# GpSimd's transfers framed as one packet per DMA engine in a short-sequence attention kernel

## The chip, the cores and the metric

The kernel runs on one core of a Trainium2 chip. The metric is the device time of one execution in microseconds (us). A core has five engines with a queue of instructions each: TensorE (PE) for matmuls, VectorE (DVE), ScalarE (ACT), GpSimd (POOL) and SyncE (SP). Data is moved between HBM and the core's memory (SBUF) by 16 DMA engines. A transfer is asked for by an instruction in the queue of GpSimd or of SyncE. It is then cut into packets on the 16 DMA engines, and a semaphore is raised when each of them is done.

## The reference

There are 32 x 12 = 384 heads of attention with a sequence of 128 and a head dimension of 64, in float32:

```python
scores = scale * np.matmul(q, k.transpose(0, 1, 3, 2))
scores_max = np.max(scores, axis=-1, keepdims=True)
attn = np.exp(scores - scores_max)
attn = attn / (np.sum(attn, axis=-1, keepdims=True) + 1e-8)
return np.matmul(attn, v).astype(np.float32)
```

The kernel reads 37.75 MB (q, k, v in float32), writes 12.58 MB, and converts q, k and v to bfloat16 in the transfer itself. It takes the exponential without subtracting the maximum, and divides at the end.

## The kernel before, in words

**Units.** Eight heads are a unit; there are 48 units. Four units are a super-unit, of which there are 12 (`supers`). Each super-unit has one load of q, one of k, and one of v (a group of v, `vgroups`), each of 1 MB in HBM and 0.5 MB in SBUF.

**Loads.** [...] A row of q or k that goes to one partition is 4096 bytes in HBM and 2048 in SBUF, 256 such rows a load. A row of v is 2048 bytes in HBM and 1024 in SBUF, 512 of them a load. q and k have four buffers each (`NQ`), v has two (`NVB`). So the load of a group of v waits until PE has read the group two before it (L396), and a load of q or k waits until DVE has copied out the one four before it (L406).

**Compute.** For each super-unit DVE pairs rows of q or k (`pair_up`, L250), PE transposes them (L177), and DVE copies the result out of PSUM (L259). PE puts v in the order of its heads (`order_v`, L191), and ACT copies it (`keep_v`, L236). For each unit PE computes the scores (L217), ACT takes the exponential (L241), PE multiplies by v with a column of ones beside it (L228), and DVE takes the reciprocal of the sums (L269) and multiplies (L272). The wait for a load of v sits on ACT, in the copy before the group's first (`v_landing`, L317 and L327).

**Stores.** Outputs are gathered one or two units at a time; a store instruction moves 256 KB. The first 34 units' stores (`own`, L365) are issued by GpSimd (34 transfers), the rest by SyncE (14 transfers), at L384 and L387. A store of two units has two pieces.

**Order.** GpSimd's queue is written out by hand (L446 to L461): loads are sorted by the step that needs them, and after each load of k some stores follow. In a settled round it holds a load of v, one of k, two to four store transfers and a load of q. All of GpSimd's transfers go through one DMA queue. SyncE's stores go through another, on the same 16 DMA engines; they are held back until unit 40 is done (`HELD`).

Of the kernel before, what the change touches and what calls it, by code (L numbers as in the profile page):

```python
# [10 lines left out]
def kernel(  # L11
# [29 lines left out]
    def slabs(t, r):  # L41
        x = t.rearrange("b h s d -> (b h s) d")
        return x.rearrange("(n p r) d -> p n (r d)", p=128, r=r)
# [3 lines left out]
    v_rows, o_rows = slabs(v, RV), slabs(out, RO)  # L47
# [34 lines left out]
    NQ, NVB, NVE, NP, NT, NA = 4, 2, 8, 4, 2, 4  # L82
# [7 lines left out]
    def sb(name, shape, dtype):  # L90
        return ctx.enter_context(nc.sbuf_tensor(name, shape, dtype))
# [9 lines left out]
    v_b = [sb(f"v_b{i}", [128, 4, RV * D], bf16) for i in range(NVB)]  # L101
# [27 lines left out]
    def op(engine, key, emit, deps=(), marks=(), dma=()):  # L129
        o = Op()  # L130
        o.key, o.emit, o.deps, o.marks, o.dma = key, emit, deps, marks, dma
        assert key not in position, key
        position[key], engine_of[key] = len(program[engine]), engine
        program[engine].append(o)

    def counts():
        c = {}
        for name, e in MARKS.items():
            n, at = 0, []
            for o in program[e]:  # L140
                n += name in o.marks
                at.append(n)
            c[name] = at
        return c
# [140 lines left out]
    s_o = [tc.alloc_semaphore(f"s_o{i}") for i in range(8)]  # L285
# [74 lines left out]
    def pieces(c):  # L360

        first = sum(stores[:c])
        return 2 if 1 < stores[c] < supers[of_unit[first]][0] // 4 else 1

    own = [c for c in range(len(stores)) if sum(stores[:c + 1]) <= OWN]  # L365

    def lane(c):

        return c % 4 + (4 if c in own else 0)

    def store(c):
        name = "POOL" if c in own else "SP"
        e = ENGINE[name]
        n = stores[c]
        first = sum(stores[:c])
        R, f = supers[of_unit[first]]
        J = R // 4

        def emit():
            dst = o_rows[:, 2 * f:2 * f + 2 * J, :].rearrange("p (a w) e -> p a w e", a=2)[  # L380
                :, :, first - f:first - f + n, :]
            src = o_sb[c][:].rearrange("p (a w e) -> p a w e", a=2, w=n)
            if pieces(c) == 1:
                e.dma_start(out=dst, in_=src).then_inc(s_o[lane(c)], 16)  # L384
            else:
                for a in range(2):
                    e.dma_start(out=dst[:, a], in_=src[:, a]).then_inc(s_o[lane(c)], 16)  # L387

        last = first + n - 1
        op(name, ("store", c), emit, [("N", last if c in own else max(last, HELD))])  # L390

    def pool_load(kind, x):
        deps = []
        if kind == "v":
            if x >= NVB:
                deps = [("V", sum(vgroups[:x - NVB + 1]) - 1)]  # L396
            n, first = vgroups[x], sum(vgroups[:x])
            op("POOL", ("load", kind, x), lambda: nc.gpsimd.dma_start(  # L398
                out=v_b[x % NVB][:, :n, :], in_=v_rows[:, first:first + n, :],
            ).then_inc(s_v[x % NVB], 16), deps)  # L400
            return
        R, f = supers[x]
        j = "qk".index(kind)
        rows, bufs, sm = ((q_rows, q_b, s_q), (k_rows, k_b, s_k))[j]
        if x >= NQ:
            deps = [("P", t) for t in t_order if t[0] == x - NQ and t[1] == j]  # L406
        n = f * 8 // R

        def emit():
            nc.gpsimd.dma_start(  # L410
                out=bufs[x % NQ][:], in_=rows[R][:, n:n + 2, :]).then_inc(sm[x % NQ], 16)

        op("POOL", ("load", kind, x), emit, deps)

# [41 lines left out]
    for _, kind, x in loads:  # L456
        pool_load(kind, x)
        while kind == "k" and sum(stores[:todo[0] + 1]) <= MIXED * (x - 4) / (len(supers) - 5):
            store(todo.pop(0))
    for c in todo:  # L460
        store(c)  # L461

    c = counts()
# [143 lines left out]
```

## Time and profile before

| | |
|---|---|
| median of 4 executions | 132.86 us (132.22 to 134.71) |
| the profiled execution | 135.14 us, of which the span of its instructions is 133.4 us |
| busy PE, DVE, ACT, POOL | 96.4, 90.9, 73.8, 51.2 us |
| GpSimd's DMA queue | 15584 packets, 27.79 MB written |
| SyncE's DMA queue | 3808 packets, 3.67 MB written |
| HBM | 37.75 MB read, 12.58 MB written |

The profile counts a transfer's bytes where they are written. A load that converts reads twice as many bytes from HBM as it writes to SBUF, so 210 GB/s in a stretch of loads is 420 GB/s at the source. A store reads and writes the same number. "DMA share" is the mean share of time in which packets of the 16 engines were open. Packets on one engine overlap, so it can go over 1.

### The profile page before, as it was taken

Reading aid. Unit: us, or ns where it says so; the run is one execution under the profiler, and the core shown is the slowest. Engines: PE = TensorE matmul, PEld = TensorE weight load, DVE = VectorE, ACT = ScalarE, POOL = GpSimd, SP = SyncE. Lnnn points to the kernel's source line nnn. Section 1 sums busy time; section 2 is a strip of 40 time slices with the busy share of each in tenths; the row PEclk is TensorE's granted clock in tenths of the full one; section 3 lists DMA queues with packets and bytes.
Section 4 is the critical chain, followed back from the end, with each engine's and each line's share of the span. In section 5 each row is a group of like instructions: output and inputs, shape, how many; then the busy total and the mean of one; then the engine's idle time right before and its main releaser. Section 6 shows DMA issues by size and latency. Waiting matters only on the chain. (4 is left out here: it accounts for less than half of the span.)

```text
span 133.4 us, 7089 instructions
## 1 busy us (share of the span) xinstructions
PE 96.4 (72%) x3072; PEld 68.5 (51%) x3072; DVE 90.9 (68%) x214; ACT 73.8 (55%) x97; POOL 51.2 (38%) x75
## 2 busy tenths in 40 slices
PE   0045779885989999769668769698499698887500
PEld 0034457564667776556446546476367466655300
DVE  1154447994698999849929839969656868876810
ACT  0001548538567877287187187486267387778500
POOL 5950006042009077491640590690930697000000
PEclk9999999999599999999999999999968999999975
DMA  2999999999999999999999999999999999999960
GB/s 17 170 198 208 210 211 210 209 211 209 207 213 170 159 269 211 210 358 215 213 355 217 212 286 209 257 317 209 252 323 208 246 321 337 403 338 337 325 227 10
DMA packets 19400, 31.56 MB, mean 237 GB/s; under 512 B 1344, under 2 KB 11072, under 8 KB 19392
## 3 DMA queue, kind: packets, MB, share of 16 engines
q0 software_dynamic: 15584, 27.79, 96.9%
q1 hardware_dynamic: 3808, 3.67, 8.1%
q8 instruction: 4, 0.07, 0.2%
q14 instruction: 4, 0.03, 0.1%
HBM read 37.75 MB, written 12.58 MB: 377 GB/s over the span
## 5 line engine op out<-in xcount | busy, mean ns | idle before, releaser
L241 ACT ACTIVATE attnT<-s_ps 128x1024 bf16<-128x1024 f32 x48 | 49.4, 1030 | 0.4 <-PE s_ps L217 0.3
L236 ACT CAST v_e<-v_ps 128x512 bf16<-128x512 f32 x48 | 28.2, 588 | 38.4 <-DMA v_b<-in_v_dram 19.6
L177 PE MATMUL qk_ps<-ident,pair 128*128 128x128 bf16 x384 | 31.9, 231 | 14.6 <-PEq L478 14.4
L191 PE MATMUL v_ps<-v_b,sel 128*32 128x256 bf16 x768 | 31.4, 286 | 13.1 <-PEq L478 13.1
L272 DVE TENSOR_TENSOR o_sb<-o_ps,recip 128x512 f32<-128x512 f32 (+1 forms) x53 | 34.0, 642 | 4.8
L259 DVE COPY qkT<-qk_ps 128x1024 bf16<-128x1024 bf16 x48 | 32.8, 684 | 5.6 <-PE qk_ps L177 4.6
L177 PEld LDWEIGHTS qk_ps<-ident,pair 128*128 128x128 bf16 x384 | 24.1, 103 | 19.8 <-issue 17.4
L398 POOL DMA_DIRECT2D v_b<-in_v_dram x12 | 9.5, 794 | 59.8 <-PE v_ps L191 59.8
L191 PEld LDWEIGHTS v_ps<-v_b,sel 128*32 128x32 bf16 x768 | 16.8, 98 | 19.5 <-issue 15.2
L228 PE MATMUL o_ps<-v_e,attnT 128*32 128x65 bf16 x1536 | 22.5, 199 | 1.7 <-PEq L478 1.1
L387 POOL DMA_DIRECT2D out_dram<-o_sb x32 | 22.9, 728 | 0.0
L269 DVE RECIPROCAL recip<-o_ps 128x8 f32<-128x8 f32 (+1 forms) x53 | 10.5, 199 | 17.6 <-PE o_ps L228 16.9
L228 PEld LDWEIGHTS o_ps<-v_e,attnT 128*32 128x32 bf16 x1536 | 16.5, 97 | 7.6 <-issue 3.4
L217 PE MATMUL s_ps<-qkT 64*128 64x128 bf16 x384 | 19.5, 222 | 0.8 <-PEq L478 0.6
L217 PEld LDWEIGHTS s_ps<-qkT 64*128 64x128 bf16 x384 | 11.1, 95 | 11.1 <-issue 11.1
L250 DVE COPY pair<-q_b 128x1024 bf16<-128x1024 bf16 x24 | 11.0, 458 | 5.5 <-DMA q_b<-in_q_dram 5.4
L250 DVE COPY pair<-k_b 128x1024 bf16<-128x1024 bf16 x24 | 10.2, 427 | 0.0
L410 POOL DMA_DIRECT2D q_b<-in_q_dram x12 | 9.0, 747 | 1.0 <-SPq L96 1.0
L410 POOL DMA_DIRECT2D k_b<-in_k_dram x12 | 8.6, 720 | 0.0
L236 ACT ACT_TABLE_LOAD x1 | 1.3, 1283 | 12.8 <-DMA v_b<-in_v_dram 12.8
L564 DVE COPY sel<-ident 128x128 bf16<-128x128 bf16 x2 | 0.4, 223 | 1.8 <-POOL ident L539 1.8
L384 POOL DMA_DIRECT2D out_dram<-o_sb x2 | 1.5, 744 | 0.0
(8 smaller groups left out, 1.4 us busy)
## 6 DMA issues: line engine op xcount, KB each, us to landing
out_dram<-o_sb POOLq DMA_DIRECT2D x34, 256.0 KB, 11.1
q_b<-in_q_dram POOLq DMA_DIRECT2D x12, 512.0 KB, 13.9
k_b<-in_k_dram POOLq DMA_DIRECT2D x12, 512.0 KB, 12.8
v_b<-in_v_dram POOLq DMA_DIRECT2D x12, 512.0 KB, 10.5
out_dram<-o_sb SPq DMA_DIRECT2D x14, 256.0 KB, 4.6
```

What stands on the lines that cost most here:

```text
L177: i = nc.tensor.transpose(p[:, :, r4, jj, :], x[:, r].rearrange("p a d -> p (a d)"), ident[:])
L191: x = nc.tensor.matmul(t[r4 * 32:(r4 + 1) * 32, i, :, :], lhsT=pick[:, w * nh + i, jv, :], rhs=v_b[g % NVB][:, :n, (4 * jv + r4) * D:(4 * ...
L217: i = nc.tensor.matmul(t[:, a, h, :], lhsT=x[p, 1, 4 * w + h, :], rhs=x[p, 0, 4 * w + h, :], start=True, stop=True)
L228: y = nc.tensor.matmul(t[h * SO:(h + 1) * SO, a, r * (D + 1):(r + 1) * (D + 1)], lhsT=x[:, a, h, r * SO:(r + 1) * SO], rhs=v_e[m % NVE][:, ...
L236: return nc.scalar.copy(v_e[m % NVE][:, :, :D], v_ps[:].rearrange("p (n e) -> p n e", e=D))
L241: return nc.scalar.activation(out=attnT[u % NA][:].rearrange("p a h (r s j) -> p (a h r) s j", r=4, j=J), in_=s_ps[u % 2][:].rearrange("p ...
L250: return nc.vector.tensor_copy(pair[t_index[t] % NP][:], src[:, 8 * b:8 * b + 8])
L259: return nc.vector.tensor_copy(x.rearrange("p h (r j s) -> p (h r) j s", r=4, j=J)[:, :, 2 * b:2 * b + 2, :].rearrange("p x j s -> p x (j ...
L269: nc.vector.reciprocal(r, o4[:, :, :, D]).then_inc(s_r, 1)
L272: return nc.vector.tensor_mul(o[:, :, w, :].rearrange("p a (r d) -> p a r d", d=D), o4[:, :, :, :D], r.unsqueeze(3).to_broadcast([128, o4. ...
L387: e.dma_start(out=dst[:, a], in_=src[:, a]).then_inc(s_o[lane(c)], 16)
L410: nc.gpsimd.dma_start(out=bufs[x % NQ][:], in_=rows[R][:, n:n + 2, :]).then_inc(sm[x % NQ], 16)
```

## The change

`dma_start` takes an argument, `single_packet`: all that one transfer has on a DMA engine is framed as one packet. It is set for GpSimd's stores (all 34), for the loads of q and k from the fifth super-unit on (16 of 24), and for the groups of v from the fourth on (9 of 12). The first four super-units of q and k and the first three groups of v keep the framing that they have. SyncE's 14 stores keep it too. No instruction, wait, buffer or order changes.

```diff
     def store(c):
         name = "POOL" if c in own else "SP"
         e = ENGINE[name]
+        how = {"single_packet": True} if c in own else {}
...
             if pieces(c) == 1:
-                e.dma_start(out=dst, in_=src).then_inc(s_o[lane(c)], 16)
+                e.dma_start(out=dst, in_=src, **how).then_inc(s_o[lane(c)], 16)
             else:
                 for a in range(2):
-                    e.dma_start(out=dst[:, a], in_=src[:, a]).then_inc(s_o[lane(c)], 16)
+                    e.dma_start(out=dst[:, a], in_=src[:, a], **how).then_inc(s_o[lane(c)], 16)
...
             op("POOL", ("load", kind, x), lambda: nc.gpsimd.dma_start(
-                out=v_b[x % NVB][:, :n, :], in_=v_rows[:, first:first + n, :],
+                out=v_b[x % NVB][:, :n, :], in_=v_rows[:, first:first + n, :], single_packet=x >= 3,
             ).then_inc(s_v[x % NVB], 16), deps)
...
             nc.gpsimd.dma_start(
-                out=bufs[x % NQ][:], in_=rows[R][:, n:n + 2, :]).then_inc(sm[x % NQ], 16)
+                out=bufs[x % NQ][:], in_=rows[R][:, n:n + 2, :], single_packet=x >= 4).then_inc(sm[x % NQ], 16)
```

## The prediction

> **What bounds the kernel now.** I read the page's rows by slice first.
>
> ```profile
> DMA  2999999999999999999999999999999999999960
> GB/s 17 170 198 208 210 211 210 209 211 209 207 213 170 159 269 211 210 358 215 213 355 217 212 286 209 257 317 209 252 323 208 246 321 337 403 338 337 325 227 10
> q0 software_dynamic: 15584, 27.79, 96.9%
> q1 hardware_dynamic: 3808, 3.67, 8.1%
> ```
>
> The DMA engines are full from 3 us to about 128 us, nearly all of it with GpSimd's queue. No compute engine is above 72%. In pure loads the rate is 208 to 213 GB/s written, so 416 to 426 GB/s read, and slices with more stores show more only because a store's bytes count once. The chain of waits reaches back only to 124 us, so I took the list of waits next.
>
> ```profile
> POOL v_b L398 <- PE v_ps L191: 59.8, 10, 12.0
> ACT v_e L236 <- DMA v_b<-in_v_dram: 19.6, 9, 3.2
> DVE pair L250 <- DMA q_b<-in_q_dram: 5.4, 3, 3.1
> ```
>
> ACT waits for a group of v nine times, at most 3.2 us: about once a round. GpSimd's 59.8 us of idle time is the buffer wait that spaces the rounds; its last six v loads start at 47.35, 55.35, 64.57, 74.80, 84.60, 93.58 and 104.52 us, a round of 57.17 / 6 = 9.53 us. Then I asked ACT's timeline where the waiting for loads ends.
>
> ```profile
> 106.06 0.59 ACT L236 CAST v_e<-v_ps 128x512 bf16<-128x512 f32 x1 [2.14 <-DMA v_b<-in_v_dram]
> ...
> 121.35 0.59 ACT L236 CAST v_e<-v_ps 128x512 bf16<-128x512 f32 x1
> ```
>
> At 106.06 us ACT takes up the copy that waited for group 10 of v (the eleventh, landed at 105.70). From there no engine waits for a load. Eight more copies come in 15.29 us, 1.91 us a unit, 7.6 us a super-unit: compute is 1.9 us a round faster than the 9.53 us of DMA. So the time is set by how soon group 10 lands, plus a tail of 21.7 us to the last multiplication at 127.39 us and the last stores behind it. The last packet lands at 131.40 us.
>
> Last, the records of single packets: each has its queue, start, duration and bytes written, and every transfer ends on each DMA engine in a 4-byte completion. On the engine that is ahead the completions of loads come 2.49 us apart where the load is q or k and 2.54 us where it is v (28.91, 31.40, 33.88, 36.42, 38.91, 41.40 us). GpSimd's stores at 114 to 117 us come 0.65 us apart, SyncE's at 121 to 126 us 0.77 us.
>
> ```
> queue   bytes written  packets  median ns  what
> GpSimd  2048           6144     173        q, k: one 4096-byte row of HBM
> GpSimd  1024           6144      98        v: one 2048-byte row
> GpSimd  4096           2176     159        stores: four rows of 1024
> SyncE   1024           3584      46        stores: one row
> ```
>
> On one engine a load of q or k is 16 packets, a load of v 32, a GpSimd store 4, a SyncE store 16.
>
> **The change, part by part.** *Loads.* q or k and v move the same bytes; v takes 2.54 - 2.49 = 0.05 us more for 16 more packets, about 3.3 ns a packet (2.487 us is the mean of the intervals before rounding). If that is a price per packet, one packet in place of 16 saves 15 x 3.3 = 50 ns a load of q or k, and one in place of 32 saves 31 x 3.3 = 102 ns a load of v.
>
> *Stores.* A SyncE store moves the same 16 KB an engine in 16 packets that GpSimd's moves in 4: 0.77 - 0.65 = 0.12 us for 12 packets, 10 ns each. That is an upper end, as the queue differs as well; 3.3 ns is the lower. Three packets fewer save 30 or 10 ns a store.
>
> *Sum to group 10's landing.* Ahead of it, or it itself: 8 loads each of q (4 to 11), 7 of k (4 to 10), 8 of v (3 to 10), 20 stores. 15 x 50 + 8 x 102 = 1.57 us, and 20 x 30 = 0.60 or 20 x 10 = 0.20 us. Together 2.17 or 1.77; I take 2.0 us. Against the profiled execution: 135.14 - 2.0 = 133.1 us. Its span was 133.4 and 1.7 us lie around it; it is 2.3 us above the median of the runs, and it holds a stretch, 41 to 48 us, of which the row below shows 162 GB/s written where 211 is usual, some 7 x 49 / 211 = 1.6 us lost. I don't carry that loss to the others and take the same 2.0 us off the median: 130.9 us.
>
> ```profile
> 41.00:48.00 7.00, 6.82 (x250) 4.85 (x241) 6.61 (x16) 5.38 (x9) 3.02 (x5) 1.00 1.06 162
> ```
>
> *The tail.* Behind group 10 lie one load each of k and v and 14 stores of GpSimd: 0.05 + 0.10 + 14 x 0.03 = 0.6 us at most. I cost it at nothing, since compute (1.91 us a unit from 106 us) covers it. Where the last packets rather than DVE's last result set the end, it adds 0.6 us of gain. That is possible: the DMA engine furthest behind ends GpSimd's stores at 121.3 us, the one ahead at 117.6, and it carries 14 SyncE stores after that.
>
> *What is late next.* A round gets 2 x 50 + 102 + 4 x 30 = 0.3 us shorter, and compute has 1.9 us of room. Nothing else becomes the bound.
>
> *Waits and queues.* No wait is added or moved. Issuing costs GpSimd 0.72 to 0.79 us a transfer, at most 7 in a round (5.2 of 9.53 us); framing could make it longer or shorter by an unknown amount. Up to 3.8 us a round it is hidden in the idle time before the v load; I take nothing. The queue runs nearly dry once, at 41.4 us (v issued at 39.76, first packet 1.6 us later): if a packet must be complete before any of it moves, up to one issue, 0.75 us, is lost there. I take nothing, and keep it in the range.
>
> *Turns between queues.* [...] Instruction loads are the one other traffic before SyncE's stores: the records show them at 2.6, 9.1, 14.7, 20.4, 37.0, 61.4, 93.9 and 97.4 us, 0.3 to 1.4 us each. The first four lie beside transfers whose framing stays (the last of them lands at 27.6 us). [...] I take nothing, as no ACT or DVE wait in the list is without a releaser.
>
> [...]
>
> **The rivals.** *It does nothing to speak of.* Loads write one record per row, though two rows of v would fit in the 4096 bytes that a store's packet holds. Perhaps a converting transfer can't be joined, or what looks like a cost per packet is one per row, which stays. Then only stores gain, 20 x 10 to 20 x 30 ns: 132.3 to 132.7 us. For it: that store rows of 1 KB are joined and v's are not. Against it: nothing in the trace.
>
> *Slower: a gap between packets.* Now many short packets overlap on an engine (173 ns long, 155 ns apart), so the next is under way before one ends. With one packet per transfer, its 16 to 32 rows might have to be fetched and opened before it moves, once a transfer. Up to group 10 there are 43 framed transfers; the gap decides from 2.0 us / 43 = 47 ns. Bounds: nothing, as transfers follow one another now without a gap; and 0.6 us, as the first packets after an empty queue took 0.66 to 0.86 us at 3.1 us and 41.4 us against 0.17, which would be 26 us. Nearer the lower end, as the queue is not empty: at 0.1 us, 43 x 0.1 - 2.0 = 2.3 us slower, 135.2 us.
>
> *More than forecast.* The tail counts as well: 2.6 us off with both upper prices, or near 2.8; 130.1 us.
>
> **How the numbers follow.** Packets cheaper as costed, the tail's addition included: 0.6, likeliest 130.9 us. Nothing to speak of: 0.16, 132.5 us. Gap: 0.24, 135.2 us. A change within 1% (1.3 us) can't be told from none here. The forecast is 1.5% faster, so most of its case is beyond that: faster 0.54; within 1% 0.24 (0.08 of the first case, 0.14 of the second, 0.02 of the third); slower 0.22. The range goes from 129.6 (the larger gain and half a us for the price per store) to 135.0 us, which takes in the second case and gaps up to near 0.1 us.
>
> **What would show it.** Right: GpSimd's queue has fewer packets, each far longer; on the engine ahead, completions after 27 us come 2.44 us apart for all loads and 0.62 to 0.64 for stores; slices of pure loads go from 209 to 211 toward 214 GB/s; ACT's last wait for v ends some 2 us sooner, and the tail behind it stays at 21.7 us. The nothing case: packet counts of 1024 and 2048 bytes as before, spacings too. The gap: spacings above 2.49 us, a DMA share that falls below 1 between transfers, and longer waits of ACT for v. I would also be wrong if an engine showed idle time without a releaser at 37, 61 or 94 us, or if GpSimd's issue grew past 1.3 us.

## The result, and the profile after

The time did not change: 133.15 us median of 42 executions against 133.06 us of 63 before, a ratio of 1.001 (95% interval 0.9993 to 1.0028). The forecast was 130.9 us. Some executions of every kernel here come out one to three per cent slower than the rest; medians in this document are of all executions and ratios of the others alone, so a ratio is not the quotient of two medians.

The page after, rows by slice and the two DMA queues (packets, MB written, share of 16 engines):

```profile
DMA  1999999999999999999999999999999999999982
GB/s 11 174 206 210 209 212 206 209 199 212 204 212 194 168 264 219 210 353 224 210 350 227 209 289 207 235 342 196 227 348 213 220 342 251 401 382 347 312 292 75
q0 software_dynamic: 15584, 27.79, 98.0%
q1 hardware_dynamic: 3808, 3.67, 8.2%
```

GpSimd's queue has 15584 packets in its records, as before, where one packet per transfer and engine would leave far fewer, if a record is a packet. By size they are the same 6144, 6144 and 2176, with the same medians of 173, 98 and 159 ns. Pure loads run at the same 209 to 212 GB/s. On the engine that is ahead, loads land 2.49 us (q, k) and 2.54 us (v) apart, stores 0.65 us, all as before.

The list of waits and ACT's timeline after (start, duration, instruction, and the wait before it) answer to those of before, nearly line for line:

```profile
POOL v_b L399 <- PE v_ps L191: 59.9, 10, 13.4
ACT v_e L236 <- DMA v_b<-in_v_dram: 19.3, 9, 4.1
DVE pair L250 <- DMA q_b<-in_q_dram: 5.5, 2, 3.0
```

```profile
106.00 0.59 ACT L236 CAST v_e<-v_ps 128x512 bf16<-128x512 f32 x1 [1.92 <-DMA v_b<-in_v_dram]
...
121.46 0.59 ACT L236 CAST v_e<-v_ps 128x512 bf16<-128x512 f32 x1
```

ACT gets group 10 of v at 106.00 us, where it was 106.06. So neither the price of a packet nor what follows from it moved. Two questions follow. Does the frame reach the DMA engines at all? And was the rest of the prediction's reasoning, price and bound, right or wrong?

### The profile page after: what moved, and what is told of

Its sections match the earlier page's. It is cut to its first block, busy times and chain, and to the rows that moved or that the text cites. A ratio compares the mean times of both kernels' runs of the same rounds, so it can differ in the third digit from the quotient of the medians.

```text
span 131.9 us, 7089 instructions
## 1 busy us (share of the span) xinstructions
PE 98.6 (75%) x3072; PEld 69.7 (53%) x3072; DVE 91.0 (69%) x214; ACT 73.9 (56%) x97; POOL 51.3 (39%) x75
## 3 DMA queue, kind: packets, MB, share of 16 engines
q0 software_dynamic: 15584, 27.79, 98.0%
q1 hardware_dynamic: 3808, 3.67, 8.2%
## 5 line engine op out<-in xcount | busy, mean ns | idle before, releaser
L177 PE MATMUL qk_ps<-ident,pair 128*128 128x128 bf16 x384 | 32.7, 234 | 13.7 <-PEq L479 13.6
L191 PE MATMUL v_ps<-v_b,sel 128*32 128x256 bf16 x768 | 32.5, 294 | 12.3 <-PEq L479 12.1
L177 PEld LDWEIGHTS qk_ps<-ident,pair 128*128 128x128 bf16 x384 | 24.7, 104 | 19.0 <-issue 16.5
```

The costliest lines, as they stand in the source:

```text
L177: i = nc.tensor.transpose(p[:, :, r4, jj, :], x[:, r].rearrange("p a d -> p (a d)"), ident[:])
L191: x = nc.tensor.matmul(t[r4 * 32:(r4 + 1) * 32, i, :, :], lhsT=pick[:, w * nh + i, jv, :], rhs=v_b[g % NVB][:, :n, (4 * jv + r4) * D:(4 * ...
```

## The experiments

**Is there a frame? Transfers alone, with and without it.** Two kernels without attention have seven stages each, every stage begun when the one before has landed. They differ in one flag on all of GpSimd's transfers. A DMA engine's turns between two queues are a test that doesn't lean on how packets are recorded. It leans instead on an engine's finishing a frame before it turns to the other queue. That was my assumption: the unframed run shows turns of one row for loads and of about four for GpSimd's stores, and no run shows longer ones.

```diff
 [(load_q, i) for i in R(0, 5)],                          # GpSimd alone
 [(load_v, i) for i in R(0, 5)],
 [(load_q, 5)] + [(store_p, i) for i in R(0, 14)],
 [(load_q, i) for i in R(6, 11)],                         # beside 9 stores of SyncE
 [(load_v, i) for i in R(5, 10)],                         # beside 9 stores of SyncE
 [(load_q, 11)] + [(store_p, i) for i in R(14, 22)],      # beside 8 stores of SyncE
 [(load_r, i) for i in R(0, 20)],                         # rows of 256 bytes
-ONE = False     # single_packet of every dma_start of GpSimd
+ONE = True
```

> Transfers alone, no attention: seven stages, each begun when the one before has landed. Five loads of q by GpSimd; five of v; one load of q and 14 stores by GpSimd; five loads of q beside nine stores of SyncE; five of v beside nine stores of SyncE; a load of q and eight stores of GpSimd beside eight of SyncE; 20 loads of 7 rows of 256 bytes a partition. Nothing is framed as one packet. Both theories: the spacings of before (2.49, 2.54, 0.65 us a transfer on one DMA engine), and beside SyncE's stores the two queues take turns row by row (q, v) or 4096 bytes by 1024 (stores): GpSimd's loads 1.3 to 1.6 times as far apart as alone.

> The same seven stages with all of GpSimd's transfers framed as one packet. Theory 'the frame is there, and what costs 3.3 ns is the row, not the packet': alone the spacings stay at 2.49, 2.54 and 0.65 us, but beside SyncE's stores the engine leaves GpSimd's queue only at a transfer's end, so SyncE's queue moves one row of 1024 bytes for each 16 to 32 rows of GpSimd's and hardly gets on until GpSimd's queue is empty (under 10 of its 144 rows an engine in that time). Theory 'the flag does nothing on this path': every stage as without it, turns included. My prediction's theory, a price per packet: 2.44, 2.44 and 0.62 to 0.64 us alone. Rows of 256 bytes: clearly shorter in the third, the same in the second.

They took 144.95 and 145.21 us, one execution each. Stretches of the seven stages, unframed first (columns: stretch, its length, busy DVE and POOL, clock, DMA share, GB/s written):

```profile
8.00:16.00 8.00, 0.00 (x0) 0.00 (x0) 1.00 1.12 211
28.00:33.00 5.00, 0.00 (x0) 0.00 (x0) 1.00 1.24 206
42.00:46.00 4.00, 0.00 (x0) 3.50 (x5) 1.00 1.03 397
54.00:68.00 14.00, 0.00 (x0) 0.23 (x1) 1.00 1.12 236
80.00:92.00 12.00, 0.00 (x0) 0.00 (x0) 1.00 1.18 246
106.00:110.00 4.00, 0.00 (x0) 0.00 (x0) 1.00 1.05 409
121.00:131.00 10.00, 0.00 (x0) 10.00 (x12) 1.00 1.92 123
```

The same stretches, framed:

```profile
8.00:16.00 8.00, 0.00 (x0) 0.00 (x0) 1.00 1.12 211
28.00:33.00 5.00, 0.00 (x0) 0.00 (x0) 1.00 1.24 205
42.00:46.00 4.00, 0.00 (x0) 3.54 (x5) 1.00 1.03 402
54.00:68.00 14.00, 0.00 (x0) 0.17 (x1) 1.00 1.12 236
80.00:92.00 12.00, 0.00 (x0) 0.00 (x0) 1.00 1.18 246
106.00:110.00 4.00, 0.00 (x0) 0.00 (x0) 1.00 1.04 405
121.00:131.00 10.00, 0.00 (x0) 10.00 (x12) 1.00 1.94 124
```

Each stage is the same within 1.3%. The turns decide it. From the completion records on one engine:

```
beside SyncE's stores        unframed: GpSimd / SyncE     framed: GpSimd / SyncE
q (16 rows a load)           3.33 us / 3.33 us            3.33 us / 3.34 us
v (32 rows a load)           4.20 us / 2.1 to 2.4 us      4.19 us / 2.1 to 2.2 us
GpSimd stores (4 packets)    0.83 us / 2.9 us             0.82 us / 2.7 to 2.9 us
```

A store of SyncE's is 16 rows. With and without the frame, 16 rows of q take as long as 16 of SyncE's, so row goes against row. That the turns are single rows, and not 16 against 16, the starts of the packets show: in each 0.2 us from 58 to 60 us 14 to 16 packets of either queue start, on 16 engines that are some 0.2 us apart, where turns of 16 rows would come in bursts of up to 2.5 us. 32 rows of v take as long as two SyncE stores, and it is one to one again. Had a load been one packet, and turns gone by packets, SyncE's queue would have stood nearly still beside it. GpSimd's stores were joined by four rows already: a store takes 0.83 us and 16 rows of SyncE's 2.9, so four to five of SyncE's rows (0.83 / 2.9 x 16 = 4.6) pass beside its four packets. The flag makes no larger packet of them. The stage with rows of 256 bytes, where a price per packet would weigh most, runs at 123 and 124 GB/s. It can't tell of that price: GpSimd issues for 10.00 of its 10.00 us, so the issue sets its pace. It shows only that the issue is no faster or slower with the flag.

The theory that the flag does nothing on this path stands; "the frame is there, only the row costs" falls because of the turns, as far as that assumption holds. A frame that the engines hold and that changes neither turns nor spacings nor records would not show here.

**All loads framed.** If frames were real, and an engine finished one before it turned, the exception for early loads would matter.

```diff
-single_packet=x >= 3     (v)      -single_packet=x >= 4     (q, k)
+single_packet=True                +single_packet=True
```

> After, with the early loads framed too (all 36 loads, 34 stores). If frames are real, an instruction load waits up to 2.5 us for its turn: the loads at 2.6, 9 to 20 us end later or PE waits longer in the first 25 us, and the time is 0 to 3 us longer than before. If the flag does nothing: 133.1 us, within 0.3%.

Measured: 133.24 us against 133.36, ratio 1.0019 (0.9987 to 1.005). The four instruction loads of queue q8 come at 3.1, 9.3, 15.0 and 20.4 us and take 0.89 to 0.96 us, where they came at 2.6, 9.1, 14.7 and 20.4 us and took 0.89 to 1.44. None is held up by the 2.5 us of a whole load. The exception for early loads parts two things that run the same.

The profiles of two such kernels also show how far single executions differ. ACT takes up group 10 of v at 104.09 us here, and at 106.00 us after:

```profile
104.09 0.59 ACT L236 CAST v_e<-v_ps 128x512 bf16<-128x512 f32 x1 [2.08 <-DMA v_b<-in_v_dram]
```

About half of this comes from the stretch of 41 to 48 us, here first and then after, where the prediction counted 1.6 us lost in the profile of before (162 GB/s):

```profile
41.00:48.00 7.00, 6.84 (x249) 4.85 (x250) 6.54 (x15) 5.48 (x8) 3.05 (x5) 1.00 1.15 234
41.00:48.00 7.00, 6.68 (x243) 4.86 (x235) 6.51 (x16) 5.35 (x8) 3.05 (x5) 1.00 1.11 186
```

So a difference of up to 2 us between two profiles in when group 10 lands says little by itself. Spacings, and times over many executions, say more.

**SyncE's stores framed too.**

```diff
-how = {"single_packet": True} if c in own else {}
+how = {"single_packet": True}
```

> After, with SyncE's 14 stores framed as one packet too. If frames save a price per packet there (10 ns each by my upper end), SyncE's stores come 0.62 us apart in place of 0.77 and the time falls by up to 1 us. If they aren't what costs: 0.77 us and 133.1 us, within 0.3%.

Measured: 133.32 us, ratio 0.9991 (0.9961 to 1.002). SyncE's queue has 3808 packets again, and the time is unchanged, so the flag is inert on this queue as well. Its stores come 0.75 to 0.78 us apart where they follow one another closely, but that spacing is no test, and the prediction misread it. SyncE issues them at this pace in before (start, us in all, five issues):

```profile
120.29 3.79 SPq L387 DMA_DIRECT2D out_dram<-o_sb  x5
```

That is 0.76 us each, and each store's first completion follows its issue by some 1.7 us: on the engine ahead the DMA waits for SyncE. The transfers alone show the DMA's own pace. There SyncE had issued nine stores by 58.15 us:

```profile
50.43 7.72 SPq L49 DMA_DIRECT2D out_dram<-src  x9
```

GpSimd's last packet there starts at 70.45 us. The stores that were left are done at 70.26, 70.94, 71.63 and 72.31 us on the engine ahead, 0.68 us apart. GpSimd's come 0.65 us apart. The 12 packets more cost 0.03 us, some 2.5 ns each, not the 10 ns that the prediction put as its upper end.

**Would fewer rows have paid? Long rows.** The prediction read 3.3 ns a packet from v against q. In the loads of before each row is a packet (16 an engine for q and k, 32 for v), so fewer rows are a way to fewer packets. This loads the same bytes as one row of 8192 bytes to a partition, with the data in other places than attention needs, so its result is attention of shuffled data.

```diff
+    q_long, k_long, v_long = slabs(q, 32), slabs(k, 32), slabs(v, 32)
...
-                out=v_b[x % NVB][:, :n, :], in_=v_rows[:, first:first + n, :],
+                out=v_b[x % NVB][:].rearrange("p n e -> p (n e)"), in_=v_long[:, x, :],
...
-                out=bufs[x % NQ][:], in_=rows[R][:, n:n + 2, :]).then_inc(sm[x % NQ], 16)
+                out=bufs[x % NQ][:].rearrange("p a e -> p (a e)"), in_=(q_long, k_long)[j][:, x, :]).then_inc(sm[x % NQ], 16)
```

> Before, unframed, with each load of q, k and v as one row of 8192 bytes to a partition: the same bytes in a half (q, k) and a quarter (v) of the rows. The rows land in other places than attention needs, so it computes attention of shuffled data; all instructions and waits are the same. If the row or its packet costs 3.3 ns: 2.46 us a load on one DMA engine, 23 x 0.026 + 11 x 0.079 = 1.5 us less up to group 10 of v, and if the DMA is the bound as I said, 1.5 us off the time (-1.1%). If rows of 8192 bytes are cut at 4096: 0.6 us off. If less DMA time does not reach the end: the spacing falls and the time stays at 133.2 us.

Measured: 131.10 us against 133.49, ratio 0.9822 (0.9776 to 0.9869): faster by 1.8%. All loads land 2.46 us apart on one engine, to the hundredth what was expected. Its queues, ACT's last wait for a group of v that starts a tail (group 10), and GpSimd's issues by line:

```profile
q0 software_dynamic: 7904, 27.79, 91.1%
q1 hardware_dynamic: 3808, 3.67, 8.3%
```

```profile
103.47 0.59 ACT L237 CAST v_e<-v_ps 128x512 bf16<-128x512 f32 x1 [1.91 <-DMA v_b<-in_v_dram]
```

```profile
L399 POOL DMA_DIRECT2D v_b<-in_v_dram x12 | 7.0, 585 | 63.3 <-PE v_ps L192 63.3
L411 POOL DMA_DIRECT2D q_b<-in_q_dram x12 | 6.9, 572 | 1.0 <-SPq L97 1.0
```

This is the picture that the frame should have given: half the packets, the same bytes, and group 10 taken up at 103.47 us in place of 106.00 (after) and 104.09 (all loads framed). From there to DVE's last multiplication, which ends at 125.04 us, are 21.6 us; after has 21.55 (106.00 to 127.55). So the tail is no shorter or longer, though ACT now waits for a load inside it (1.44 us for group 11, at 111.95 us).

The gain in time is 2.4 us (1.7 to 3.0 by the interval), more than the 1.5 us forecast. One cause is an issue that the sum lacked: GpSimd issued a load of 8 rows an engine in 0.54 to 0.59 us, where it took 0.72 to 0.79 with 16 and 32, and the first load lands 0.33 us sooner than after. The engine ahead ends group 10 at 100.50 us in place of 102.84, 2.34 us sooner, of which spacing by rows accounts for 1.5. The last engine, on which ACT waits, ends it 2.54 us sooner. What is left over can't be told apart from what single executions differ by.

**The other direction: short rows.** q and k in rows of 1024 bytes, 64 to an engine.

```diff
+    q_short, k_short = slabs(q, 4), slabs(k, 4)
...
-                out=bufs[x % NQ][:], in_=rows[R][:, n:n + 2, :]).then_inc(sm[x % NQ], 16)
+                out=bufs[x % NQ][:].rearrange("p a (c e) -> p (a c) e", c=4), in_=(q_short, k_short)[j][:, 8 * x:8 * x + 8, :]).then_inc(sm[x % NQ], 16)
```

> Before, unframed, with q and k loaded in rows of 1024 bytes, 64 to a DMA engine in place of 16 (v as before; the data is shuffled likewise). If a row costs 3.3 ns: 2.65 us a load of q or k, 23 x 0.16 = 3.6 us more up to group 10, and 3.6 us on the time if the DMA is the bound (+2.7%). If slack takes it up: less than 1 us on the time.

Measured: 137.74 us, ratio 1.0345 (1.027 to 1.042). Loads of q and k land 2.66 us apart (2.65 expected), 6144 packets have become 24576, and ACT takes up group 10 at 109.02 us:

```profile
109.02 0.59 ACT L237 CAST v_e<-v_ps 128x512 bf16<-128x512 f32 x1 [1.99 <-DMA v_b<-in_v_dram]
```

```profile
L411 POOL DMA_DIRECT2D q_b<-in_q_dram x12 | 11.1, 926 | 1.1 <-SPq L97 1.1
L411 POOL DMA_DIRECT2D k_b<-in_k_dram x12 | 10.9, 906 | 0.0
```

From 8 to 64 rows the price is (2.66 - 2.46) / 56 = 3.6 ns a row. The time rose by some 4.6 us (3.45% of 133.5) against 3.6 by rows, which lies at the end of the interval (1.027); here too the issue changed with the rows, to 0.91 and 0.93 us.

**Stores in long rows.** Two rows of 1024 bytes become one of 2048 (the output's places are shuffled).

```diff
+    o_long = slabs(out, 8)
...
-                    e.dma_start(out=dst[:, a], in_=src[:, a]).then_inc(s_o[lane(c)], 16)
+                    e.dma_start(out=o_long[:, (2 * f + J * a + first - f) // 2, :], in_=o_sb[c][:, 512 * a:512 * a + 512]).then_inc(s_o[lane(c)], 16)
```

> Before, with the stores of two units written as one row of 2048 bytes in place of two of 1024 (the output's places are shuffled). If what parts SyncE's 0.77 us from GpSimd's 0.65 is the row (10 ns each): SyncE's come 0.69 us apart and GpSimd's 0.57 to 0.65, and the time falls by 0 to 1.5 us. If it is the queue: SyncE's stay at 0.77 us and the time within 0.3%.

Measured: 132.53 us, ratio 0.995 (0.9922 to 0.9977), about 0.7 us. SyncE's stores come 0.65 us apart in place of 0.77 where they follow closely. As 0.77 was SyncE's issue, this is not a gain of 0.12 us by rows; against the 0.68 us of such stores alone it is 0.03 us for 8 fewer, some 4 ns each. Nor can this part row from packet, since on SyncE's queue each row is a packet (16 of 1024 bytes a store in before). GpSimd's stores keep their 2176 packets of 4096 bytes and come 0.63 us apart in place of 0.65. There the rows were halved and the packets kept, and 0.02 us by 8 rows is 2.5 ns each: a hint that the price goes with the row, but no more than the rounding of the two figures allows. GpSimd's issue of these stores fell too, from 0.73 to 0.57 us. Which of these the 0.7 us comes from was not taken apart.

**GpSimd's joined stores for all.** If GpSimd's stores took 0.65 us of an engine and SyncE's 0.77, more stores on GpSimd would be less DMA work at the end.

```diff
-    MIXED, OWN, HELD = 24, 34, NU - 8
+    MIXED, OWN, HELD = 24, 46, NU - 8
```

> Before, unframed, with all stores but the last two issued by GpSimd (12 transfers of 256 KB move from SyncE's queue to GpSimd's, where four rows share a packet). If the tail is bound by DMA: 12 x 0.12 = 1.4 us less of it, up to 1.4 us off the time. If compute covers the tail, as I costed it in the prediction: within 0.3% of before, or up to 1 us more, as GpSimd takes 0.72 us to issue a store.

> The same with the last two stores on GpSimd too. Their way from issue to landing decides: about 1.5 us from GpSimd's issue to a first packet when its queue is empty (1.49 to 3.03 us at the start), against SyncE's shorter one: 0.5 to 1 us slower than with the last two on SyncE.

Measured: with 46, 134.28 us, ratio 1.0062 (1.0023 to 1.01), slower. With 48 (`OWN` 48, and SyncE's waits for lanes without a store left out), 135.17 us, ratio 1.0201 (1.0127 to 1.0276). The expected 1.4 us was never there: by the stores alone, 0.68 against 0.65 us, it is 12 x 0.03 = 0.4 us. What the loss is made of stands in SyncE's waits at the end of the program (before, 46, 48), each a wait for the other engines to reach their end. The name in the row is not the one that it waits for:

```profile
SPq L533 <- PEq L533: 0.2, 1, 0.2
SPq L533 <- PEq L533: 1.0, 1, 1.0
SPq L533 <- PEq L533: 2.1, 1, 2.1
```

GpSimd ends last with 46 and 48. Its closing drain ended 2.4 and 2.5 us after the last packet of its queue (at 132.88 and 131.37 us). In before it ended at 123.69 us, also 2.4 us after, and was long over when SyncE's last store landed. So 46 costs 0.8 us more of waiting than before, as much as its 0.6%. With 48 it is 1.9 us of the 2.7 that 2.0% makes; the rest is not explained, and with four executions the interval is wide. The step from 46 to 48 was expected to cost 0.5 to 1 us by the stores' way to landing; its waiting alone costs 1.1 us, and lies behind the landing.

No kernel here with its data in the right places beats both before and after. The long rows point to one, but a row of 8192 bytes puts other rows of v and q on a partition than the reordering on PE expects. I did not rebuild that.

## Why the prediction was wrong, by its own steps

**What bounds the kernel: right.** The DMA engines set the time up to the landing of group 10, and a tail of compute and the last stores follows. Long rows take 1.5 us of DMA by their spacing up to there and 2.4 us off the time; short rows add 3.6 us and 4.6 us. That loads land when the spacings say was borne out, and the tail kept its length (21.3, 21.6 and 21.6 us from ACT's copy of group 10 to DVE's last multiplication in before, after and long rows).

**The price of a load's packet: right in size, and a price of the row as much as of the packet.** 3.3 ns was read from q against v, and by that figure 2.46 and 2.65 us were forecast for kernels that had not been run; 2.46 and 2.66 were measured. But in every load here a row is a packet, so no run parts the two, and the prediction took the one for the other. The upper price of a store, 10 ns, was a misreading: 0.77 us was the pace of SyncE's issue, and the 0.68 us of the stores alone gives 2.5 ns. The lower one, 3.3 ns, was near.

**The step that failed** is the one from the flag to the packets: "one packet in place of 16 saves 15 x 3.3 = 50 ns a load of q or k, and one in place of 32 saves 31 x 3.3 = 102 ns a load of v", and three packets fewer a store. It was taken from what the flag is said to do, and no row of the profile showed that it would. The packets stayed 16, 32 and 4 (15584 on GpSimd's queue before and after), so 1.57 us for loads and 0.2 to 0.6 for stores were 0. "If that is a price per packet" was never put to the test.

The rival "It does nothing to speak of" had it right for the loads, and I gave it 0.16 and put the case against it as nothing in the trace. The row that spoke for it was there: v's two rows of 2048 bytes were not joined though stores were joined up to 4096. That is a hint and no proof: four rows of a store lie side by side in HBM, while rows of v that go to one partition do not. In that rival even the stores were to gain 0.2 to 0.6 us, and they gained nothing.

**The rival of a gap between packets** did not come about: no larger packet shows. Spacings and the DMA share are as before. The same holds for instruction loads waiting for a turn, as far as the records show: the four beside framed transfers took 0.31 to 0.32 us each, as before.

**The tail, costed at nothing: not tested by this change,** since its 14 stores kept their packets. In the profiles the last packet lands 2.4 us (after) to 4.0 us (before) behind DVE's last result, so stores do set the end, as the prediction held possible. Stores in long rows brought 0.7 us; how much of it fell ahead of group 10 (some 20 x 0.02 = 0.4 us by spacing) and how much behind was not separated.

**Issue, costed at nothing: right for this change** (0.72 to 0.80 us a load before and after), but it isn't fixed. It changed with the number of rows (0.54 to 0.59 us with 8 an engine, 0.91 to 0.93 with 64), and that is a part of the long rows' gain that the sum lacked.

What stays open: whether the flag is dropped on its way to the DMA engines or reaches them and is ignored. The program carries it on 59 transfers (34 + 16 + 9); the runs show only that packets, turns, spacings and issue times are as without it.

## What to carry to other kernels

An edit that sets a flag has a step ahead of all its prices: that the flag is acted on. Look for a row in the profile that shows it acting before working out what it saves, and test it alone by something that it should change; here, how two queues take turns on one DMA engine. When DMA is the bound, count the rows of a transfer: in this kernel each row of a load cost 3.3 to 3.6 ns an engine, and a load of q or k took 0.54 to 0.57 us to issue with 8 rows an engine and 0.91 to 0.93 with 64; lengthening rows gave 1.8% where framing them gave nothing. Before a spacing is read as the price of a transfer, see that the DMA engine was not waiting for the issue.

## What the runs showed of the hardware

- In the transfers alone a DMA engine took turns between GpSimd's and SyncE's queues row by row for loads (3.33 us for 16 rows of each), and after about four rows of 1024 bytes for GpSimd's stores (0.83 us a store beside 2.9 us), whatever the flag said.
- A store of 256 KB in rows of 1024 bytes took a DMA engine 0.68 us from SyncE's queue (16 packets) and 0.65 us from GpSimd's (4 packets), each with nothing beside it.
- GpSimd's closing drain ended 2.2 to 2.5 us after the last packet of its queue (before, after, 46 and 48 stores); with 46 stores on GpSimd the time was 0.6% longer, with 48 2.0%.
- GpSimd's time to issue a load of 1 MB followed its rows: 0.54 to 0.59 us with 8 rows an engine, 0.72 to 0.75 with 16, 0.91 to 0.93 with 64; but 0.79 with the 32 rows of v.
- Around 41 to 48 us, where GpSimd's queue has nearly run dry, executions with the same transfers lose differently: 162, 186 and 234 GB/s written in before, after and all loads framed, with packets of up to 0.95, 0.90 and 0.81 us. Why is open.
